# Opening of a one-level Strassen matmul with GELU: A11's first part as two halves, the first product over all row tiles per half of B12

## The chip, the cores and the metric

The kernel runs on one core of a Trainium2 chip. A core has TensorE for matrix products (PE, with PEld for its weight loads), VectorE (DVE), ScalarE (ACT), GpSimd (POOL) and SyncE (SP); POOL and SP issue the DMA transfers here. The metric is the device time of one execution in microseconds, lower is better, as the median of several runs.

## The reference

```python
def reference(a, b):                 # a, b: 4096 x 4096, float32, normal random
    x = np.matmul(a, b)
    return 0.5 * x * (1 + np.tanh(np.sqrt(2 / np.pi) * (x + 0.044715 * x**3)))
```

One product of 4096 x 4096 x 4096 and the tanh form of GELU on each element; the output is float32.

## The kernel before, in words

The operands are cast to fp16 on their way in and the products are accumulated in float32. Both matrices are cut into quadrants of 2048 x 2048, named by two digits: for A, "12" is the upper rows and the second half of the contraction; for B, the first half of the contraction and the right columns. The output is computed in 16 groups; a group is 512 rows and 512 columns of each of the four output quadrants. Instead of eight quadrant products most of the work uses seven products of sums and differences (`PRODUCTS`), and later groups use a second level of the same trick.

The first group is different, because nothing is on chip when it starts. For the first half of each quadrant's contraction (1024 of 2048, part 0) it computes the eight quadrant products plainly, in the order of `PLAIN`; for part 1 it uses the seven products. So the steps of the first group are 16 plain half steps (`plain(n)`, n = 0 to 15) and then 14 steps of `multiply` (line 581 is their matmul). A plain quadrant product is 512 x 512 outputs over 1024 of contraction: four row tiles i = 0 to 3 of 128 rows, each with eight matmuls of 128 x 128 by 128 x 512 (line 629), so 32 matmuls. The eight slices of the contraction are named (j, e), j = 0 to 3 and e = 0 or 1. A product is cut into its two half steps either by e (four matmuls for each of the four row tiles, then the other four) or, where `by_rows` is true, by row tiles.

What the opening has to bring in is written out by hand as words in a list (lines 731 to 750), each word under the number of the step before which it is issued:

- `A11_0` loads part 0 of A's quadrant 11 into a staging tile (`stage`), `B12_0` loads part 0 of B's quadrant 12 into its `bR` tile. All these loads are issued by POOL (line 485), in the order of the list. A load of an A part is 16 blocks of 32 rows; a load of a B part is two halves, e = 0 and e = 1.
- A suffix a or b is the first or second half (for A: row blocks 0 to 7 or 8 to 15; for B: e = 0 or e = 1), and p, q, r, s are quarters of A's row blocks (r: 8 to 11, s: 12 to 15). Every such piece is four DMA transfers, one for each 32 partitions. A half of either is 4 transfers of 128 KB, a quarter of A is 4 transfers of 64 KB (written bytes).
- `T11_0` transposes the staged rows into the `aT` tile on DVE (line 458); a suffix does it for these rows only. Row tiles 0 and 1 need T11_0a, row tile 2 needs T11_0r, row tile 3 needs T11_0s.
- `W11_0` squares and adds up the staged rows on ACT (line 494) for a guard on the numbers' size, in place, so it runs after the transposes, and the staging tile is free for the next load only after it.

The order of the words sets the order on each engine's queue; waits between engines come from what an instruction reads and writes. POOL also waits before an issue when too many of its transfers are under way (the planner of the later groups counts with `LANES = 8` on a queue).

Before the first product `warm()` runs `N_WARM` matmuls on zeros (line 590), so that TensorE is busy while the first data come in. In `plain`, the first product (n = 0 and 1: A11 by B12, output quadrant 12) has an order of its own: in n = 0 row tiles 0 to 2 take the four e = 0 slices, in n = 1 row tiles 0 to 2 take the four e = 1 slices, and then row tile 3 takes all eight. n = 2 and 3 are A11 by B11, n = 4 and 5 A21 by B11 (by rows), n = 6 and 7 A21 by B12 (by rows). When a product's accumulators are complete ACT copies them out (`keep`, line 599), or DVE adds them (line 595). The sums for `multiply` are made by DVE at line 566 (`make_sums`), two steps ahead.

From the second group on, a planner (`Plan`) orders all instructions at build time from fixed costs; the change does not touch its input.

Of the kernel before, what the change touches and what calls it, by code (L numbers as in the profile page):

```python
# [22 lines left out]
RT = 4  # L23
# [21 lines left out]
C21_FIRST = (0, 5, QPH - 1)  # L45
M5_FIRST = (1, 2, QPH - 1)
THIRD = ("22", 1)
N_WARM = 33

SQUARE_MAX = 2.0**22  # L50
SQUARE_MIN = 2.0**-6
# [295 lines left out]
def half_path(  # L347
# [225 lines left out]
    def bank(s, i):  # L573
        return PS[s][i][:, :]
# [11 lines left out]
    def warm():  # L586
        z = cell(sum_cells[0])
        nc.vector.memset(z[:, :NC], 0.0)
        for _ in range(N_WARM):
            nc.tensor.matmul(  # L590
# [3 lines left out]
    def tt(o, x, y, op):  # L594
        nc.vector.tensor_tensor(out=o, in0=x, in1=y, op=op)

    def keep(tag, src):
        t = ring(tag)[:, :]
        nc.scalar.copy(out=t, in_=src)
        return t  # L600

    def plain(n):

        (quad, oa, ob, by_rows), h = PLAIN[n // 2], n % 2
        seen = [x for x in range(len(PLAIN)) if PLAIN[x][0] == quad]
        sa, sb = a_phys[a_slot[oa], 0], b_phys[b_slot[ob], 0]
        sa = sa.rearrange("p jj (m e) -> p jj m e", e=2)
        tiles = [(j, e) for j in range(NJ // 2) for e in range(2)]
        odd = [[t for t in tiles if t[1] == e] for e in range(2)]
        rows = range(h * RT // 2, (h + 1) * RT // 2)  # L610
        if n == 0:
            pieces = [(i, odd[0]) for i in range(RT - 1)]
        elif n == 1:
            pieces = [(i, odd[1]) for i in range(RT - 1)] + [(RT - 1, tiles)]
        elif by_rows:
            pieces = [(i, tiles) for i in rows]
        else:
            pieces = [(i, odd[h]) for i in range(RT)]
        for i, part_ in pieces:
            begins, ends = part_[0] == tiles[0], part_[-1] == tiles[-1]  # L620
            acc = bank(0 if quad == "11" else 1, i)
            kept = quad == "11"
            start = (n // 2 == seen[0] or quad in ("12", "21")) and begins
            stop = (n // 2 == seen[-1] or not kept) and ends
            c = f"c{quad}"
            if quad == "22" and n // 2 == seen[1]:
                nc.scalar.copy(out=acc, in_=post.pop((c, i)))
            for j, e in part_:
                nc.tensor.matmul(
                    acc, sa[:, j, i * P : (i + 1) * P, e], sb[:, 2 * j + e, :],  # L630
                    start=start and (j, e) == part_[0], stop=stop and (j, e) == part_[-1],
                    skip_group_check=True,
                )
            if not stop:
                continue
            if quad in ("12", "21") and n // 2 == seen[1]:
                tt(post[c, i], post[c, i], acc, ALU.add)
            elif quad == "12":
                post[c, i] = keep("x1", acc)
            elif quad == "11":  # L640
                tt(post["c12", i], post["c12", i], acc, ALU.add)
            elif quad == "21":
                post[c, i] = keep("c21", acc)
            elif n // 2 == seen[0]:
                post[c, i] = keep("y", acc)
            else:
                tt(post["c12", i], post["c12", i], acc, ALU.subtract)
# [81 lines left out]
    before = {}  # L729

    for n, whats in (
        (0, "A11_0a B12_0a A11_0r B12_0b A11_0s T11_0a T11_0r T11_0s W11_0 B11_0 A21_0 A12_0 B22_0 B21_0"),
        (4, "T21_0 W21_0 A22_0"),
        (6, "T12_0 W12_0:0-8"),
        (8, "W12_0:8-16"),
        (10, "B12_1 A11_1 B22_1"),
        (11, "T22_0 W22_0 A12_1"),
        (13, "T11_1 A22_1 B21_1"),
        (16, "W11_1 B11_1"),
        (16, "T12_1"),  # L740
        (17, "A21_1"),
        (18, "T22_1 S2 W22_1:0-4"),
        (19, "W22_1:4-8"),
        (20, "W22_1:8-12"),
        (21, "W22_1:12-16"),
        (23, "T21_1"),
        (position[2, 2], "N11_0"),
        (position[3, 2], "N21_0"),
        (position[3, 3], "N11_1"),
        (position[4, 3], "N21_1"),  # L750
    ):
        for what in whats.split():
            half = what[-1] == "0" and what != "A11_0" and what[0] != "N" or what in ("A22_1", "T22_1")
            if what[0] == "S":
                before.setdefault(n, []).append((make_sums, (2, int(what[1]), "bS")))
                continue
            if what[0] == "N":
                before.setdefault(n, []).append((load, [(load_b1, (what[1:3], int(what[4])))]))
                continue
            if what[0] == "W":  # L760
                xs = range(*(int(x) for x in what[6:].split("-"))) if what[6:] else range(NX)
                before.setdefault(n, []).append((weigh_first, (what[1:3], int(what[4]), xs)))
                continue
            for h in (0, 1) if half else (None,):
                args = [
                    (x[0], (x[1:3], int(x[4]), x[5] if x[5:] in tuple("pqrs") else "ab".index(x[5]) if x[5:] else h))
                    for x in what.split("+")
                ]
                if what[0] == "T":
                    before.setdefault(n, []).append((turn_a, args[0][1]))  # L770
                    if what == "T22_1":
                        for q in range(QPH // 2, QPH):
                            before[n].append((make_sums, (2, q, "aS", h)))
                else:
                    pairs = [({"A": load_a, "B": load_b}[x], xs) for x, xs in args]
                    before.setdefault(n, []).append((load, pairs))

    def first_group():
        warm()
        table = pool.tile([P, 1], F32, name="table", tag="table")  # L780
        nc.vector.memset(table[:, :], 0.0)
        nc.scalar.activation(table[:, :], table[:, :], ACT.Gelu_apprx_tanh)
        for n, step in enumerate(steps):
            for fn, args in before.get(n, ()):
                fn(*args)
            if n + AHEAD < len(steps):
                s, q = steps[n + AHEAD]
                if s >= 0 and (0, *step) != C21_FIRST and (s, q) != M5_FIRST[1:]:
                    make_sums(s, q)
            if step[0] != 2:  # L790
                flush()
            combine()
            if step == (NP - 1, QPH // 2):
                for i in range(RT):
                    products(bank(0, i), *first_operands(), True, True, i)
            if step[0] < 0:
                plain(n)
            else:
                multiply(*step)
            if (0, *step) == C21_FIRST and n + AHEAD < len(steps):  # L800
                make_sums(*steps[n + AHEAD])
            if step == (2, QPH - 1):
                flush()
        flush()
        combine()
# [1352 lines left out]
def kernel(tc: tile.TileContext, a: bass.AP, b: bass.AP, out: bass.AP):  # L2158
    stands = half_path(tc, a, b, out)
    with tc.If(stands == 0):  # L2160
        general_path(tc, a, b, out)
# [30 lines left out]
```

## Time and profile before

| | before |
|---|---|
| median of 3 runs | 1450.55 us (1448.99 to 1450.82) |
| the profiled execution | 1450.24 us |
| its span in the trace | 1448.7 us |
| PE busy | 1436.2 us (99% of the span) |
| DVE / ACT / POOL busy | 1212.5 / 706.5 / 486.7 us |
| granted TensorE clock, mean | 1.00 |

The profiled execution is 0.31 us under the median of the runs, and 1.5 us of it lie outside the span. The views used below are: the page with its totals; PE's timeline, in which a row is a run of instructions with its start, its length, the count and, in brackets, how long the engine had been idle before and what ended that; the chain of waits, the work that ended last followed back from the end; the tables of busy time by window; and the list of DMA issues. A matmul's recorded time reaches to its modelled end, past the start of the next one, so a run of n matmuls takes (n - 1) spacings and one full record.

### The profile page before, as it was taken

How to read it: one execution, taken by the hardware profiler on the slowest of the kernel's cores; microseconds unless marked ns; L12 is line 12 of the kernel's file. 1: busy time of each engine (PE TensorE's matmuls, PEld its weight loads, DVE VectorE, ACT ScalarE, POOL GpSimd, SP SyncE). 2: the span in 40 equal slices, each digit the busy share in tenths (PEclk: the TensorE clock that was granted, in tenths of full speed). 3: DMA queues.
4: the chain of work that ended last, by engine and by line, in shares of the span. 5: the costliest groups of instructions: out<-in, count | busy, mean ns of one | idle time of the engine just before them, and what ended most of it. 6: DMA issues, size and time to landing. Idle time of an engine off the chain costs nothing.

```text
span 1448.7 us, 20127 instructions
## 1 busy us (share of the span) xinstructions
PE 1436.2 (99%) x6961; PEld 680.2 (47%) x6961; DVE 1212.5 (84%) x1315; ACT 706.5 (49%) x1480; POOL 486.7 (34%) x892
## 2 busy tenths in 40 slices
PE   8999999999999999999999999999999999999998
PEld 3444454564544545444444444444444444444443
DVE  2498988986878779989998989887998889887876
ACT  5645865455885543562655413453463622343133
POOL 8765251343244523331323343222322213111120
PEclk9999999999999999999999999999999999999999
DMA  9999999999999999998989899979898867775773
GB/s 160 195 218 241 300 267 276 245 276 255 235 241 246 259 286 234 285 286 285 307 289 323 262 311 320 290 221 343 225 345 251 303 224 265 281 267 204 268 257 116
DMA packets 205245, 378.94 MB, mean 262 GB/s; under 512 B 21072, under 2 KB 115792, under 8 KB 205136
## 3 DMA queue, kind: packets, MB, share of 16 engines
q0 software_dynamic: 146816, 245.42, 69.9%
q1 hardware_dynamic: 58320, 132.15, 24.3%
q8 instruction: 57, 0.93, 0.3%
q14 instruction: 52, 0.43, 0.1%
HBM read 333.45 MB, written 138.42 MB: 326 GB/s over the span
## 4 chain that ended last, share of the span: by engine, by line
PE 93%; DMA 3%; POOL 2%; DVE 1%; issue 1%; ACT 0%; DVEq 0%; POOLq 0%
PE acc L1857 58%; PE acc L581 30%; PE acc L1030 5%; DMA stage<-in_a_dram 2%; DMA bR<-in_b_dram 1%; POOL bR L485 1%; POOL stage L485 1%; DMA bR<-k_unit 0%; DVE y L1303 0%; DVE bR L945 0%; ACT stage L494 0%; DVE y L1388 0%; DVE aD L566 0%; POOL aD L485 0%; ACT y L2026 0%
## 5 line engine op out<-in xcount | busy, mean ns | idle before, releaser
L1857 PE MATMUL acc<-bR 128*128 128x512 f16 x1536 | 339.4, 379 | 0.9 <-DVE bR L945 0.9
L945 DVE TENSOR_TENSOR bR<-bR 128x2048 f16<-128x2048 f16 (+1 forms) x159 | 263.6, 1672 | 35.4 <-PE acc L1857 22.7
L826 POOL DMA_DIRECT2D bR<-k_unit x234 | 126.7, 543 | 491.0 <-PE acc L1857 364.1
L1857 PEld LDWEIGHTS <-bR 128*128 128x128 f16 x1776 | 173.5, 98 | 210.8 <-issue 1.1
L581 PE MATMUL acc<-bR,aT 128*128 128x512 f16 x1088 | 239.7, 379 | 0.9 <-DVE y L1303 0.9
L1857 PE MATMUL acc<-bR,aT 128*128 128x512 f16 x1008 | 223.6, 379 | 0.0
L1857 PEld LDWEIGHTS <-aT 128*128 128x128 f16 x1344 | 131.3, 98 | 158.8
L1869 ACT COPY acc<-acc 128x512 f32<-128x512 f32 x140 | 79.8, 570 | 245.8 <-PE acc L1857 229.6
L1303 DVE TENSOR_TENSOR y<-acc,y 128x512 f32<-128x512 f32 x251 | 166.2, 686 | 39.9 <-PE acc L1857 17.5
L826 POOL DMA_DIRECT2D bR<-in_b_dram x256 | 137.9, 544 | 180.8 <-PE acc L581 60.3
L581 PE MATMUL acc<-bR,aD 128*128 128x512 f16 x832 | 180.9, 379 | 0.0
L581 PEld LDWEIGHTS <-aT 128*128 128x128 f16 x1152 | 112.5, 98 | 132.6 <-issue 1.4
L1383 ACT ACTIVATE y<-bR 128x1024 bf16<-128x1024 f16 x128 | 130.6, 1051 | 70.4 <-DVE y L1388 62.7
L581 PEld LDWEIGHTS <-aD 128*128 128x128 f16 x928 | 90.6, 98 | 110.9 <-DVE aD L566 1.7
L1857 PE MATMUL acc<-bR,aD 128*128 128x512 f16 x624 | 138.4, 379 | 0.0
L1281 ACT ACTIVATE y<-y 128x512 f32<-128x512 f32 x160 | 98.4, 629 | 67.5 <-DVE y L1303 67.1
L1857 PEld LDWEIGHTS <-aD 128*128 128x128 f16 x784 | 76.6, 98 | 92.6
L1866 ACT COPY y<-acc 128x512 f32<-128x512 f32 x99 | 57.8, 585 | 93.3 <-PE acc L1857 87.8
L1388 DVE TENSOR_TENSOR y<-y 128x1024 bf16<-128x1024 bf16 x120 | 82.5, 688 | 23.8 <-ACT y L1383 22.4
L458 DVE STREAM_TRANSPOSE aT<-stage 128x1024 uint32<-128x1024 uint32 (+2 forms) x42 | 52.6, 1278 | 35.9 <-DMA stage<-in_a_dram 35.9
L1857 PE MATMUL acc<-stage,aT 128*128 128x512 f16 x336 | 75.6, 379 | 0.0
L826 POOL DMA_DIRECT2D stage<-in_a_dram x80 | 46.3, 586 | 69.6 <-ACT stage L1339 20.2
(124 smaller groups left out, 1670.8 us busy)
## 6 DMA issues: line engine op xcount, KB each, us to landing
bR<-k_unit POOLq DMA_DIRECT2D x234, 512.0 KB, 7.7
out_dram<-y SPq DMA_DIRECT2D x204, 256.0 KB, 7.1
bR<-in_b_dram POOLq DMA_DIRECT2D x352, 128.0 KB, 6.0
k_unit<-bR SPq DMA_DIRECT2D x76, 512.0 KB, 6.3
stage<-in_a_dram POOLq DMA_DIRECT2D x92, 256.0 KB, 9.7
stage<-k_unit POOLq DMA_DIRECT2D x46, 512.0 KB, 7.9
k_unit<-stage SPq DMA_DIRECT2D x28, 512.0 KB, 5.3
out_dram<-bR SPq DMA_DIRECT2D x46, 256.0 KB, 7.5
```

Of the source, the lines that this page charges most:

```text
L458: nc.vector.transpose(dst[:, :, x, :], src)
L581: nc.tensor.matmul(acc, sa[:, j // 2, i * P : (i + 1) * P, j % 2], sb[:, j, :], start=start and j == 0, stop=stop and j == 3, skip_group_c ...
L826: return plan.add(queue, COST[queue], lambda: eng.dma_start(out=dst, in_=src), r=r, w=w, size=MOVE[what] * SPREAD, weight=weight, **kw)
L945: nc.vector.tensor_tensor(out=dst, in0=xa, in1=ya, op=ALU.add if op > 0 else ALU.subtract)
L1030: nc.tensor.matmul(PS[s][i][:, :] if wide else PS[s][i][:, w * HC : (w + 1) * HC], sa[:, j // 2, r * P : (r + 1) * P, j % 2], rhs(j, wide) ...
L1281: act("gelu", lambda: nc.scalar.activation(t, t, ACT.Gelu_apprx_tanh), [("f", f)], [("f", f)])
L1303: dve("add", lambda: nc.vector.tensor_tensor(out=sm(g), in0=bank(s, i), in1=sm(f), op=ALU.add), [("f", f)], [("f", g), ("p", s, i)])
L1383: act("square", lambda t=t, src=src: nc.scalar.activation(t, src, ACT.Square), [c(cx)], [("f", f)], slack=60.0)
L1388: dve("add16", lambda t=t, u=u: nc.vector.tensor_tensor(out=u, in0=u, in1=t, op=ALU.add), [("f", f)], [("f", e)], slack=60.0)
L1857: nc.tensor.matmul(bank(w, i), sa[:, jx // 2, r * P : (r + 1) * P, jx % 2], bv[:, jx, :], start=p in "17" and jx == 0, stop=jx == NJ - 1, ...
L1866: act("copy", lambda: nc.scalar.copy(out=sm(f), in_=bank(w, i)), [("p", w, i)], [("f", f)])
L1869: act("copy", lambda: nc.scalar.copy(out=bank(*dst), in_=bank(*x)), [("p", *x)], [("p", *dst)])
```

## The change

Three edits.

1. The second half of A11's part 0 is loaded as one half in four transfers of 128 KB (`A11_0b`) where it was two quarters of four transfers of 64 KB each (`A11_0r`, `A11_0s`). The half stands where the first quarter stood, ahead of B12's second half; the second quarter stood behind it. The transposes keep their pieces: a half and two quarters.
2. The special order of the first product goes. n = 0 now takes the e = 0 slices for all four row tiles (16 matmuls; it was 12), n = 1 the e = 1 slices for all four (16; it was 20).
3. `warm()` issues 35 matmuls instead of 33.

```diff
-N_WARM = 33
+N_WARM = 35
...
         rows = range(h * RT // 2, (h + 1) * RT // 2)
-        if n == 0:
-            pieces = [(i, odd[0]) for i in range(RT - 1)]
-        elif n == 1:
-            pieces = [(i, odd[1]) for i in range(RT - 1)] + [(RT - 1, tiles)]
-        elif by_rows:
+        if by_rows:
             pieces = [(i, tiles) for i in rows]
         else:
             pieces = [(i, odd[h]) for i in range(RT)]
...
-        (0, "A11_0a B12_0a A11_0r B12_0b A11_0s T11_0a T11_0r T11_0s W11_0 B11_0 A21_0 A12_0 B22_0 B21_0"),
+        (0, "A11_0a B12_0a A11_0b B12_0b T11_0a T11_0r T11_0s W11_0 B11_0 A21_0 A12_0 B22_0 B21_0"),
```

## The prediction

> **What bounds the kernel now.** First the page:
>
> ```profile
> span 1448.7 us, 20127 instructions
> PE 1436.2 (99%) x6961; PEld 680.2 (47%) x6961; DVE 1212.5 (84%) x1315; ACT 706.5 (49%) x1480; POOL 486.7 (34%) x892
> PE 93%; DMA 3%; POOL 2%; DVE 1%; issue 1%; ACT 0%; DVEq 0%; POOLq 0%
> ```
>
> TensorE is busy for 99% of the span, yet 5% of the chain that ended last is DMA and POOL. So the second view is that chain, its first 85 us, and from a second answer its sequel:
>
> ```profile
> 11.70 2.13 POOL stage L485 x4
> 13.83 1.06 POOL bR L485 x2
> 14.89 5.18 DMA bR<-in_b_dram
> ...
> 42.69 1.31 ACT stage L494 x6
> ...
> 72.46 0.28 issue
> ...
> 79.43 4.17 DMA bR<-in_b_dram
> 83.61 1.24 DVE aD L566
> ```
>
> ```profile
> by line: PE acc L1857 61.5%; PE acc L581 31.7%; PE acc L1030 5.1%; DMA bR<-k_unit 0.4%; DVE y L1303 0.4%; DVE bR L945 0.2%; issue 0.1%; DVE y L1388 0.1%; DVE aD L566 0.1%; ACT y L2026 0.0%; DVEq L945 0.0%; DVEq L1388 0.0%
> ...
> 84.89 107.27 PE acc L581 x496
> ```
>
> Up to 83.61 the chain is almost only loads: POOL issues, a transfer lands, POOL issues again. From 84.89 on it is TensorE (98% of the rest), so what is won or lost at 84.89 should reach the end unchanged. The third view is PE's timeline up to there:
>
> ```profile
> 1.46 9.95 PE L590 MATMUL acc<-aD 128*128 128x512 f16 x33 [1.46 <-DVE table L781]
> 11.24 2.93 PE L629 MATMUL acc<-bR,aT 128*128 128x512 f16 x12
> 15.29 4.48 PE L629 MATMUL acc<-bR,aT 128*128 128x512 f16 x20 [1.12 <-DMA bR<-in_b_dram]
> 20.89 14.04 PE L629 MATMUL acc<-bR,aT 128*128 128x512 f16 x64 [1.12 <-DMA bR<-in_b_dram]
> 35.10 34.70 PE L629 MATMUL acc<-bR,aT 128*128 128x512 f16 x160 [0.17 <-ACT y L599]
> ...
> 76.61 7.07 PE L581 MATMUL acc<-bR,aD 128*128 128x512 f16 x32
> 84.89 13.99 PE L581 MATMUL acc<-aD 128*128 128x512 f16 x64 [1.21 <-DVE aD L566]
> ```
>
> 64 matmuls in 14.04 us are 63 spacings and one record of 0.38: 0.217 us each. A stall therefore costs its idle time plus 0.16, the part of a record that the next matmul would have covered. The costs: 0.18 inside the first twelve (2.93 instead of 11 x 0.217 + 0.38 = 2.76), 1.28 before 15.29 (waits for B12's second half), 1.28 before 20.89 (B11's first half), 0.33 before 35.10, 1.37 before 84.89 (a sum on DVE, which in the chain waits for a B load). Together 4.4 us: all that better loading can win behind the warm-up.
>
> The last one decides. Without it TensorE would go on at 83.52, so it has 1.37 us of slack against the load stream: the end moves with the moment at which the B load of 83.61 lands, not with what TensorE does at 11 to 20 us, until TensorE falls more than 1.37 us behind.
>
> **The change, part by part.** *Fewer, larger issues.* POOL's timeline and the list of issues:
>
> ```profile
> 6.13 1.11 POOL L485 DMA_DIRECT2D stage<-in_a_dram  x2
> 7.86 1.23 POOL L485 DMA_DIRECT2D stage<-in_a_dram  x2 [0.61 <-DMA stage<-in_a_dram]
> 9.20 2.50 POOL L485 DMA_DIRECT2D bR<-in_b_dram  x4
> 11.69 2.14 POOL L485 DMA_DIRECT2D stage<-in_a_dram  x4
> 13.82 4.29 POOL L485 DMA_DIRECT2D bR<-in_b_dram  x8
> 18.43 0.58 POOL L485 DMA_DIRECT2D stage<-in_a_dram  x1 [0.31 <-DMA bR<-in_b_dram]
> ```
>
> ```profile
> stage<-in_a_dram POOLq DMA_DIRECT2D x28, 128.0 KB, 5.0
> stage<-in_a_dram POOLq DMA_DIRECT2D x8, 64.0 KB, 3.8
> ```
>
> The quarters are the eight 64 KB issues at 6.13, 7.86 and 11.69, 0.535 to 0.58 us each; a 128 KB issue of the same kind took 0.58 (18.43). Four of 0.58 replace the first quarter's four (1.11 + 1.23 = 2.34), so B12's second half is still issued from about 9.2, and the four at 11.69 go: B11 and all loads behind it can be issued about 2.1 us earlier. Issue time is not landing time, so the windows:
>
> ```profile
> 8.00:10.00 2.00, 2.00 (x11) 0.93 (x10) 1.25 (x1) 0.34 (x2) 1.64 (x4) 1.00 1.25 192
> 10.00:15.00 5.00, 4.17 (x19) 1.52 (x17) 0.71 (x1) 4.66 (x24) 4.78 (x10) 1.00 1.20 165
> 15.00:20.00 5.00, 4.48 (x20) 1.88 (x20) 0.71 (x1) 2.50 (x10) 4.27 (x8) 1.00 1.06 144
> 20.00:30.00 10.00, 9.11 (x43) 4.17 (x44) 1.25 (x1) 3.67 (x16) 7.14 (x13) 1.00 1.38 193
> 30.00:84.00 54.00, 53.51 (x247) 23.82 (x245) 31.30 (x34) 33.92 (x146) 41.00 (x74) 1.00 1.32 196
> ```
>
> (Columns: window, length, busy us of PE, PEld, DVE, ACT and POOL with counts, granted clock, DMA share, GB/s.) From 20 us on the stream runs at 193 to 196 GB/s without a dip, so it is full, and a lead in bytes gained before 20 us is kept to 83.6. Between 10 and 20 us it is not full: 165 and 144 GB/s, while POOL is busy 4.78 and 4.27 of 5 us. Against 193 that is 5 x (193 - 165) + 5 x (193 - 144) = 385 KB, or 2.0 us of a full stream: the upper bound of the lead, near the 2.1 us of issue time. The lower bound is zero, and I let it go to -0.4 us, because the bytes are the same and the B11 transfers alone, eight 128 KB issues from 13.82, already meet a wait at 18.43 while the stream carries 144: there larger pieces do not fill it. I take the share that belongs to the quarters. 64 KB in 0.535 us is 122 GB/s; over 2.14 us that is (193 - 122) x 2.14 = 152 KB or 0.8 us short. The first quarter's issues are as slow, but the stream held 192 at 8 to 10 us, from what was queued; I add 0.2 us for them. **The lead: 1.0 us** (estimate from these rows).
>
> *The order of the bytes, and the first product.* B12's second half now has 262 KB more ahead of it, the second quarter's. The transposes and the T21 that matters later:
>
> ```profile
> 8.38 1.25 DVE L458 STREAM_TRANSPOSE aT<-stage 128x1024 uint32<-128x1024 uint32 x1 [6.97 <-DMA stage<-in_a_dram]
> 12.37 0.71 DVE L458 STREAM_TRANSPOSE aT<-stage 128x512 uint32<-128x512 uint32 x1 [2.74 <-DMA stage<-in_a_dram]
> 16.76 0.71 DVE L458 STREAM_TRANSPOSE aT<-stage 128x512 uint32<-128x512 uint32 x1 [3.68 <-DMA stage<-in_a_dram]
> ...
> 30.01 1.25 DVE L458 STREAM_TRANSPOSE aT<-stage 128x1024 uint32<-128x1024 uint32 x1 [2.57 <-DMA stage<-in_a_dram]
> ```
>
> A11's whole second half lands 262 KB after the first quarter did (12.37), at 165 to 193 GB/s 1.4 to 1.6 us: 13.8 to 14.0. Its two transposes end at 14.6 and 15.3, so row tile 2 waits about 1.1 us longer than row tile 0 and 1 last (to 11.67 + 8 x 0.217 = 13.4), and row tile 3 is done at about 16.2. B12's second half now lands where the second quarter did, 16.7, less a part of the lead: 16.2 to 16.7. Sixteen matmuls of 0.217 are 3.5 us, so n = 1 ends at 19.7 to 20.2. B11's first half, 20.89 before, comes at 19.9. So n = 2 starts at 19.9 to 20.2, 0.7 to 1.0 us earlier. Nothing is lost even if B12 came as late as 17.4 (3.5 before 20.89). ACT's squares of rows 8 to 11 start about 2 us later and those of rows 12 to 15 earlier; the copies of the first product behind them are needed only by n = 4, at about 27.
>
> *Before 35.10* TensorE waits for ACT's copies of quadrant 21's accumulators:
>
> ```profile
> 34.49 2.00 ACT L599 COPY y<-acc 128x512 f32<-128x512 f32 x4
> ```
>
> They stand behind the squares of A21, which follow T21's second half, released by a load at 30.01. That moves with the stream, TensorE's own part with n = 2: both 0.7 to 1.0 earlier. The chain's step through ACT at 42.69 (a staging tile free late) follows TensorE and moves as much.
>
> *Two more warm matmuls* end 0.43 us later, 11.67 instead of 11.24, for row tiles 0 and 1 alone; row tile 2 starts when its transpose lets it. They cost nothing; if that cover went, 0.43.
>
> *The sum.* The sum on DVE ends at 84.85 - 1.0; TensorE is there at 83.52 - 0.7 or earlier, so 84.89 becomes 83.9. 1450.24 - 1.0 = 1449.24. The profiled execution lay 0.31 under the median of the runs; half of that added gives **1449.4 us**, bounds of the lead alone 1448.2 (2.0) and 1450.6 (-0.4).
>
> **Rivals.** *Hidden.* The stream is full from 20 us, and its dip at 15 to 20 may belong to B11's access and not to the quarters: the wait at 18.43 speaks for it. Then the lead is within 0.4 us and the time 1450.3: the change does not do what it says. Against it: 165 GB/s at 10 to 15, while POOL is busy 4.78 of 5.
>
> *More.* The lead is over 1.8 us, because eight full transfers under way hold 193 GB/s from 8 us on. Then TensorE's other stalls shrink too: 1448.4 down to 1450.24 - 4.4 = 1445.8 if all go. Against it: n = 1 cannot end before 19.7.
>
> *The clock drops (slower).* Place: TensorE between 13.4 and 17 us. It now waits twice close together, about 1.1 us for T11_0r and up to 0.9 us for B12, with eight matmuls (1.7 us) between. The weight loads of the warm-up show the price:
>
> ```profile
> 3.56 0.15 PEld L590 LDWEIGHTS <-aD 128*128 128x128 f16 x1 [0.28 <-issue]
> 3.99 0.15 PEld L590 LDWEIGHTS <-aD 128*128 128x128 f16 x1 [0.28 <-issue]
> ...
> 6.92 3.98 PEld L590 LDWEIGHTS <-aD 128*128 128x128 f16 x19 [0.22 <-issue]
> ```
>
> 0.43 us apart until 6.92, then 0.216. A stretch as long as from 1.46 to 6.92 at half speed costs 2.7 us. It decides once TensorE loses more than the 1.37 us of slack: with the lead of 1.0, one stretch gives about 1450.6, two 1453.3, three 1456. Against it: stalls of 1.28 at 15.29 and 20.89 left the spacing at 0.217. [...]
>
> **How the numbers follow.** The forecast (lead 0.4 to 1.8) 0.58; hidden 0.22; more 0.10, of which 0.06 below 1447.65; the clock 0.10, of which 0.06 above 1453.45. 0.2% is 2.9 us, about what a measurement of this kernel can tell from no change; 4.4 us is all there is to win, so within 0.2% has 0.88, faster 0.06, slower 0.06. The forecast's own range is 1448.4 to 1449.9. The range for 8 in 10 takes in hidden, half of more and one cold stretch, with the runs' spread of about 1: 1447.4 to 1452.0.
>
> **What would show it.** B11's issues from about 11.7 to 12 instead of 13.82; over 170 GB/s at 10 to 20 us; n = 2 at 19.9 to 20.2; 84.89 at about 83.9; and a shift of the same size at the end. Wrong: a rate of 144 again at 15 to 20, a spacing of 0.43 after 13 us, or a stall after 84.89 that is not in the trace of before.

## The result, and the profile after

The changed kernel takes 1447.69 us (median of 14 runs, 1446.58 to 1450.05), the kernel before beside it 1450.23 us. The ratio is 0.9983 with a 95% interval of 0.9976 to 0.999: about 2.5 us or 0.17% faster, less than the 0.2% that the prediction took as its bound, but the interval excludes no change. On another chip the same pair gave 1447.93 and 1449.67 us, ratio 0.9988 (0.9979 to 0.9997).

The profiled execution took 1447.74 us, its span is 1446.1 us against 1448.7. PE's timeline of the changed kernel (start, length, line, operation, count, and in brackets the idle time before and what ended it):

```profile
1.46 9.36 PE L590 MATMUL acc<-aD 128*128 128x512 f16 x35 [1.46 <-DVE table L777]
11.14 1.89 PE L625 MATMUL acc<-bR,aT 128*128 128x512 f16 x8 [0.32 <-DMA bR<-in_b_dram]
14.61 53.81 PE L625 MATMUL acc<-bR,aT 128*128 128x512 f16 x248 [1.58 <-DVE aT L458]
...
75.16 7.07 PE L581 MATMUL acc<-bR,aD 128*128 128x512 f16 x32
82.46 13.99 PE L581 MATMUL acc<-aD 128*128 128x512 f16 x64 [0.23 <-DVE aD L566]
```

The three stalls of before inside the plain products (1.12, 1.12 and 0.17 us) are gone. A new one stands in their place, 1.58 us for the transpose of row tile 2, and the first product now waits 0.32 us for B12. From 14.61 on 248 matmuls run without a gap. The matmuls that started at 84.89 start at 82.46, 2.43 us earlier, and the stall before them is down from 1.21 to 0.23 us.

The stream of loads, by the same windows as before (columns as there; the last is GB/s):

```profile
3.00:8.00 5.00, 5.00 (x20) 2.06 (x19) 0.00 (x0) 0.00 (x0) 4.91 (x9) 1.00 1.14 144
8.00:10.00 2.00, 2.00 (x11) 0.88 (x9) 1.25 (x1) 0.65 (x3) 1.18 (x3) 1.00 1.14 169
10.00:15.00 5.00, 3.10 (x14) 1.12 (x13) 1.16 (x2) 3.07 (x17) 4.11 (x8) 1.00 1.34 195
15.00:20.00 5.00, 5.00 (x24) 2.17 (x23) 0.14 (x1) 4.52 (x18) 4.28 (x9) 1.00 1.23 201
20.00:30.00 10.00, 10.00 (x48) 4.52 (x47) 2.49 (x2) 4.74 (x22) 7.85 (x15) 1.00 1.43 194
```

The stream carries 195 and 201 GB/s at 10 to 20 us, where it had been 165 and 144. From 10 us on it is as full as later (194 at 20 to 30 us); only at 8 to 10 us it carries less than before, 169 instead of 192.

The shift at 82.46 does not reach the end unchanged. PE's waits after it, in the timeline of the changed kernel:

```profile
299.51 1.02 PE L581 MATMUL acc<-bR,aT 128*128 128x512 f16 x4 [0.92 <-DVE y L1299]
694.89 3.61 PE L1853 MATMUL acc<-bR 128*128 128x512 f16 x16 [1.23 <-DVE bR L941]
899.27 3.61 PE L1853 MATMUL acc<-bR 128*128 128x512 f16 x16 [0.47 <-ACT acc L1865]
```

Before, the second of these matmuls started at 696.96 after 0.86 us of idle time. So the lead is 2.43 at 299.5, 2.07 at 694.9, and a small stall at 899.3 that was not there takes 0.6 more. The last GELU on ACT ends at 1442.30; before, at 1443.74 (1443.08 and 0.66), 1.44 us later. The span gained 2.6 because what follows the last GELU, the last stores, took 3.8 us in this execution and 4.9 in that of before. In a second profile of the changed kernel the lead was 2.61 at 299.3, 2.16 at 694.8 and 2.16 at the last GELU. So the change brings 2.4 to 2.6 us at 84.9, and later waits take 0.4 to 1.0 of it. What follows the last GELU took 3.8, 4.9 and (in the second profile) 4.4 us, half a microsecond up or down. That the time fell by 2.5 us, as much as the lead, is therefore partly chance: between the first two profiles it is 2.43 of lead, less 1.0 at the waits, plus 1.1 in the tail. On the other chip it was 1.7.

### The profile page after: what moved, and what is told of

It reads as the page before. It is cut to its first block, busy times and chain, and to the rows that moved or that the text cites. A ratio compares the mean times of both kernels' runs of the same rounds, so it can differ in the third digit from the quotient of the medians.

```text
span 1446.1 us, 20123 instructions
## 1 busy us (share of the span) xinstructions
PE 1435.4 (99%) x6963; PEld 681.3 (47%) x6963; DVE 1212.2 (84%) x1315; ACT 707.0 (49%) x1480; POOL 485.7 (34%) x888
## 4 chain that ended last, share of the span: by engine, by line
PE 93%; DMA 3%; POOL 3%; issue 1%; DVE 1%; ACT 0%; DVEq 0%; POOLq 0%
PE acc L1853 58%; PE acc L581 30%; PE acc L1026 5%; POOL bR L485 2%; DMA stage<-in_a_dram 1%; POOL stage L485 1%; DMA bR<-in_b_dram 1%; DMA bR<-k_unit 0%; DVE y L1299 0%; DVE bR L941 0%; DVE y L1384 0%; DVE aD L566 0%; ACT y L1862 0%; POOL aD L485 0%; ACT stage L494 0%
## 5 line engine op out<-in xcount | busy, mean ns | idle before, releaser
L1862 ACT COPY y<-acc 128x512 f32<-128x512 f32 x99 | 57.9, 586 | 94.6 <-PE acc L1853 83.9
L1304 DVE TENSOR_TENSOR acc<-acc,y 128x512 f32<-128x512 f32 x100 | 67.9, 690 | 2.1 <-ACT acc L1865 1.1
```

The costliest lines, as they stand in the source:

```text
L1304: dve("add", lambda: nc.vector.tensor_tensor(out=bank(s, i), in0=bank(s, i), in1=sm(f), op=ALU.add), [("f", f)], [("p", s, i)])
L1862: act("copy", lambda: nc.scalar.copy(out=sm(f), in_=bank(w, i)), [("p", w, i)], [("f", f)])
```

## The experiments

Two theories stood against each other: that the eight 64 KB transfers leave the stream of loads short (S, later made exact as Q), or that it is the order of the bytes and products (O, P), or the B11 loads themselves (B), that make the dip at 10 to 20 us.

**Edit 1 alone.**

```diff
-A11_0a B12_0a A11_0r B12_0b A11_0s T11_0a
+A11_0a B12_0a A11_0b B12_0b T11_0a
```

> Edit 1 alone: A11's second half as four 128 KB transfers ahead of B12's second half; the first product's old order and 33 warm matmuls stay. Theory S (the eight 64 KB issues starve the load stream at 10 to 20 us; the order of the products plays no part): the whole shift comes with this edit, 195 GB/s or more at 10 to 20 us, the matmuls of 84.89 start at 82.3 to 82.8, time 2.2 to 2.8 us under the kernel before. Theory P (the gain needs the new order of the first product, since TensorE releases what follows): under half of that, 84.89 becomes 83.7 or later.

Measured: 1449.16 us, the kernel before 1449.90; ratio 0.9995 (0.9985 to 1.0004). PE's timeline, and the row of the windows:

```profile
11.10 1.89 PE L629 MATMUL acc<-bR,aT 128*128 128x512 f16 x8 [0.54 <-DMA bR<-in_b_dram]
14.56 1.04 PE L629 MATMUL acc<-bR,aT 128*128 128x512 f16 x4 [1.57 <-DVE aT L458]
16.41 52.82 PE L629 MATMUL acc<-bR,aT 128*128 128x512 f16 x244 [0.82 <-DMA bR<-in_b_dram]
...
82.89 13.98 PE L581 MATMUL acc<-aD 128*128 128x512 f16 x64
```

```profile
15.00:20.00 5.00, 4.18 (x20) 1.79 (x19) 0.09 (x1) 4.47 (x18) 4.27 (x9) 1.00 1.24 201
```

The stream is full (201) with edit 1 alone, and 2.0 of the 2.43 us at 84.89 are there. But now TensorE comes last at 82.89, with no wait in front of it: in the old order there are only four matmuls between row tile 2's transpose and B12's second half, and it stands idle for another 0.82 us. The new order puts row tile 3's four matmuls there. So P, which put these matmuls at 83.7 or later, is refuted there, and edit 2 is worth 0.3 to 0.4 us at this place. The time did not follow S, though: 0.7 us were gained, not 2.2 to 2.8. Between this kernel and the one with all edits but 33 warm matmuls (below) the medians of the runs show more, 1.5 us, than the two traces do (0.3 at 82.6, 0.8 in the span). Three of this kernel's ten runs show a mean granted clock of 0.998, against one in ten there. That the two stalls of 1.57 and 0.82 close together cost clock in those executions is a guess: in this kernel's trace the granted clock is 1.00 in every window from 0 to 84 us. The other seven have a mean of 1448.9, and where their remaining 1.2 us come from stays open. (An estimate: one stretch of 3.4 us at half clock, as in the last section, lowers the mean over the span of 1447.3 us by 0.0012, so a run listed with 0.999 can hold one too.)

**Edit 2 alone.**

```diff
-        if n == 0:
-            pieces = [(i, odd[0]) for i in range(RT - 1)]
-        elif n == 1:
-            pieces = [(i, odd[1]) for i in range(RT - 1)] + [(RT - 1, tiles)]
-        elif by_rows:
+        if by_rows:
```

> Edit 2 alone: the first product over all row tiles per half of B12, with the quarters and their place as before and 33 warm matmuls. Theory S: the stream is as before, 144 GB/s at 15 to 20 us; row tile 3 waits for the transpose that ends at 17.5, n = 1 ends at about 21.8, 0.9 us later than the B11 data that was waited for; the slack of 1.37 us at 84.89 swallows it: same time within 0.4 us. Theory P: 1 us or more faster.

Measured: 1451.52 us against 1449.90, ratio 1.0013 (1.0003 to 1.0023): slower by 1.6 us. PE's timeline and two windows:

```profile
11.55 2.75 PE L625 MATMUL acc<-bR,aT 128*128 128x512 f16 x12
17.45 54.53 PE L625 MATMUL acc<-bR,aT 128*128 128x512 f16 x244 [3.15 <-DVE aT L458]
...
85.62 13.98 PE L581 MATMUL acc<-aD 128*128 128x512 f16 x64
```

```profile
15.00:20.00 5.00, 2.55 (x7) 0.96 (x8) 0.71 (x1) 1.70 (x8) 4.12 (x8) 0.77 1.16 153
20.00:30.00 10.00, 10.00 (x45) 4.40 (x44) 2.12 (x2) 4.75 (x16) 8.12 (x15) 0.94 1.39 191
```

The wait for the second quarter's transpose is where S put it (17.45), and the stream has its dip (153). That the slack of 1.37 us would swallow it was wrong, because of a thing that S left out: after a stall of 3.15 us the granted clock is 0.77 and 0.94 in the next two windows. 244 matmuls took 54.53 us instead of 243 x 0.2165 + 0.38 = 53.0; these 1.5 us came on top, and TensorE arrived after the loads. Edit 2 without edit 1 is a loss.

**33 warm matmuls.**

```diff
-N_WARM = 35
+N_WARM = 33
```

> The changed kernel with 33 warm matmuls instead of 35. If the two cost and bring nothing: within 0.3 us of the changed kernel, first product from 11.14 as there (it waited 0.32 us for B12 behind 35 of them), spacing 0.217 from there on. If they hold the clock up: matmuls at 0.43 us after 11 us, and 1 to 3 us slower.

Measured, beside the changed kernel's other edits: 1447.70 us against 1449.90, ratio 0.9984 (0.9974 to 0.9994), the changed kernel's own ratio. The first product starts at 11.24 after 0.62 us of idle time (0.32 with 35), when B12's first half is there; the later matmuls start at 82.61. Edit 3 does nothing that can be seen.

**The quarters, in the new order of bytes.**

```diff
-A11_0a B12_0a A11_0b B12_0b T11_0a
+A11_0a B12_0a A11_0r A11_0s B12_0b T11_0a
```

> The changed kernel, its order of bytes and of products, but A11's second half as two quarters of 64 KB transfers, both ahead of B12's second half: 20 issues in the opening as in the kernel before, 4 more than in the changed one. Theory S (issue time and size): the stream is slow again, 140 to 170 GB/s somewhere at 10 to 20 us, all later issues about 2 us later, 84.89's matmuls at 84.3 to 84.9, time within 0.6 us of the kernel before. Theory O (the order of the bytes fills the stream, the size does not matter): 82.3 to 82.8 and the changed kernel's time.

Measured: 1450.53 us against 1449.90, ratio 1.0003 (0.9993 to 1.0012). The gain is gone. Windows and PE:

```profile
10.00:15.00 5.00, 4.38 (x20) 1.53 (x19) 1.42 (x2) 3.97 (x21) 4.50 (x9) 1.00 1.19 154
15.00:20.00 5.00, 2.48 (x11) 1.01 (x12) 0.00 (x0) 2.27 (x11) 4.14 (x9) 0.98 1.12 164
20.00:30.00 10.00, 10.00 (x41) 4.17 (x40) 1.48 (x2) 4.18 (x15) 8.08 (x15) 0.84 1.38 195
```

```profile
18.55 53.65 PE L625 MATMUL acc<-bR,aT 128*128 128x512 f16 x240 [2.52 <-DMA bR<-in_b_dram]
...
85.85 13.98 PE L581 MATMUL acc<-aD 128*128 128x512 f16 x64
```

Order, products and warm-up are those of the changed kernel; only A11's second half differs, eight transfers of 64 KB for four of 128 KB, and the dip is back. So it is the size, not the order. The first A21 transpose starts at 26.49 where the changed kernel has 24.37: the stream is 2.1 us behind. And again a stall (2.52 us) is followed by a lower clock (0.84), which puts the 85.85 behind the 84.9 expected. The drop alone does not explain the time: the three of the ten runs with a mean granted clock of 1.00 took 1449.0 to 1450.1 us.

Why the size matters so much is seen in the landings. Each transfer posts sixteen completions in the trace. The table has some of the opening's loads, numbered in order of issue: the start of the issue, the last completion, the time since the last completion of the transfer before, and issue to landing, all in us, worked out from the traces' semaphore events.

```
                     issue   landed   since   issue to landing
before   9  64 KB     6.13    11.20    0.33    5.06
        12  64 KB     8.54    12.24    0.35    3.70
        16 128 KB    11.15    15.16    0.76    4.01
        20  64 KB    13.29    16.64    0.43    3.35
        21 128 KB    13.82    18.14    1.50    4.32
        23 128 KB    14.89    20.08    1.07    5.19
changed  1 128 KB     1.55     4.72     -      3.17   (nothing ahead of it)
        12 128 KB     8.23    13.71    0.69    5.48
        16 128 KB    11.29    16.32    0.66    5.04
        20 128 KB    14.00    18.92    0.65    4.92
        24 128 KB    16.61    21.53    0.66    4.92
quarters 9  64 KB     6.13    11.66    0.36    5.53
        16  64 KB    11.59    14.09    0.33    2.51
        17 128 KB    12.12    15.47    1.38    3.35
        19 128 KB    13.18    17.76    1.63    4.57
```

When bytes are queued, a 128 KB transfer lands 0.65 to 0.69 us after the one ahead and a 64 KB transfer 0.33 to 0.36: the same 180 to 200 GB/s. A 128 KB transfer with nothing ahead of it took 3.17 us from issue to landing, so of the changed kernel's steady 4.92 some 1.8 us are queue (an estimate, the difference). POOL needs 0.54 us to issue 64 KB that land in 0.35. Every quarter therefore eats the queue, and when issue to landing is down at 2.5 to 3.4 us the next transfers come 1.1 to 1.6 us apart instead of 0.65. In the kernel before this happens at transfer 21, the first of B11: the dip at 15 to 20 us lies in the B11 loads, but the quarters issued just ahead of them made it.

The issue time is not the only reason. In all thirteen traces POOL never has more than eight of these loads under way: each issue starts at least 0.28 us after the landing of the load eight places ahead. In the changed kernel that wait, and not the issue time, sets the pace (transfer 12 landed at 13.71, transfer 20 was issued at 14.00). Where full 128 KB transfers land every 0.65 us, a quarter can be issued only every 0.65 us, and it brings half the bytes. Transfers 11 to 16 of the run above were issued 0.64 to 1.32 us apart for this reason; in the kernel before, the quarters of 11.69 to 13.29 came every 0.53 us, at the pace of issuing. Both eat the queue. No run allows more than eight under way, so how much belongs to which stays open.

**More quarters at the start.**

```diff
-A11_0a B12_0a A11_0b B12_0b T11_0a
+A11_0p A11_0q B12_0a A11_0b B12_0b T11_0a
```

> The changed kernel with A11's first half cut into two quarters of 64 KB transfers as well: 4 more issues, at the very start. Theory Q (a queue runs dry: a 64 KB transfer lands 0.35 us after the one before it but takes 0.54 us to issue, so quarters eat what is queued, and time is lost only when nothing is left): the first product's data come 0.5 to 1.2 us later, but B12 and the later loads lose only what the queue behind them cannot make up, 0.3 to 0.9 us; 84.89's matmuls at 82.8 to 83.4. Theory I (every issue of 0.54 us delays the whole stream by itself): all loads 2.1 us later, 84.3 to 84.6, the time of the kernel before.

Measured: 1449.22 us against 1449.80, ratio 0.9994 (0.9984 to 1.0004): most of the gain is gone. From 3 to 8 us the stream carries 107 GB/s, where the changed kernel has 144. PE:

```profile
13.02 1.89 PE L625 MATMUL acc<-bR,aT 128*128 128x512 f16 x8 [1.18 <-DMA bR<-in_b_dram]
16.49 53.80 PE L625 MATMUL acc<-bR,aT 128*128 128x512 f16 x248 [1.58 <-DVE aT L458]
...
84.64 13.99 PE L581 MATMUL acc<-aD 128*128 128x512 f16 x64 [0.53 <-DVE aD L566]
```

2.2 us later than the changed kernel, Theory I's number and not the 0.3 to 0.9 that I took for Q. This need not speak against a queue that runs dry, but my use of it was wrong. At the very start nothing is queued that could make up for slow issues: the first seven transfers of 64 KB took 2.4 to 3.1 us from issue to landing, no more than one with nothing ahead of it. So there each extra issue of 0.54 us delays everything by itself. This account was made after the run.

**Quarters where the stream is full.**

```diff
-B11_0 A21_0 A12_0
+B11_0 A21_0p A21_0q A21_0r A21_0s A12_0
```

> The changed kernel with A21's loads (issued from 17 us on, when the stream is full and eight transfers are under way) as four quarters of 64 KB transfers, 8 more issues. Theory Q: sixteen issues of 0.55 us are 8.9 us for bytes that land in 5.4; the queue of about 2 us behind the floor of 3 us from issue to landing takes up a part, so the stream falls 1 to 2 us behind with a dip in GB/s at 22 to 28 us; 84.89's matmuls at 83.3 to 84.3, time 0.5 to 1.8 us over the changed kernel. Theory B (the dip belonged to the B11 loads and the opening, not to small transfers): no dip, within 0.3 us of the changed kernel.

Measured: 1451.76 us against 1449.80, ratio 1.0007 (0.9997 to 1.0017), 4 us over the changed kernel's 1447.7 to 1447.9 (on two other chips). Windows and PE:

```profile
22.00:28.00 6.00, 5.20 (x25) 2.15 (x22) 1.15 (x1) 0.00 (x0) 4.95 (x10) 1.00 0.95 110
28.00:34.00 6.00, 5.84 (x28) 2.66 (x29) 1.34 (x2) 5.87 (x29) 5.60 (x11) 1.00 1.05 124
```

```profile
28.16 38.23 PE L625 MATMUL acc<-bR,aT 128*128 128x512 f16 x176 [0.95 <-DVE aT L458]
68.42 5.30 PE L625 MATMUL acc<-bR,aT 128*128 128x512 f16 x16 [2.04 <-ACT acc L623]
...
87.57 12.69 PE L581 MATMUL acc<-aD 128*128 128x512 f16 x58
```

No B11 load and no opening here, and the dip is deeper and longer than that of the kernel before: 110 and 124 GB/s over 12 us. Issue to landing falls from 4.92 to 3.10 us within six 64 KB transfers, and then the gaps begin. These six were issued 0.65 us apart, each behind the landing eight places ahead, so here it is the limit of eight and not the issue time that emptied the queue. Theory B is refuted. The price, 5.1 us at 87.57, is more than twice the upper end of what I gave to Q, since I had counted only the issue times, and neither the limit of eight nor what happens once the queue is empty. Of the 5.1 us the loads alone are 4.4 behind at 37 us, before the clock is at half from 69.2 to 72.6 us, behind the stall of 2.04.

**Fewer warm matmuls.** Three kernels, the changed one with

```diff
-N_WARM = 35
+N_WARM = 23      # and 28, and 16
```

> The changed kernel with 23 warm matmuls: TensorE stands idle from about 8.2 to 11.1 us, some 2.9 us, the length of the stalls after which the clock was seen at half in the two runs with a stall of 2.5 and 3.1 us. If the length of one stall decides: matmuls 0.43 us apart for a while after 11.1 and a granted clock of 0.5 to 0.8 there. If it took something else: 0.217 throughout.

> The changed kernel with 28 warm matmuls: a stall of about 1.8 us before 11.1, between the 1.58 us that left the clock at 1.00 and the 2.52 us after which it fell. If the length of one stall decides: clock 1.00, the changed kernel's time within 0.6 us. If stalls that follow each other add up (1.8 and then 1.6 us): half clock after 13 us.

> The changed kernel with 16 warm matmuls, so that TensorE stands idle for 2 us or more before the first product; 1.7 us had left the clock alone, while 2.04, 2.5 and 3.1 us elsewhere were followed by some 3 us at half. If the length of one stall decides: a granted clock under 0.9 in a window behind 11 us and matmuls 0.43 us apart there, 84.89's matmuls later than in the changed kernel only if TensorE loses more than its slack. If it needs more than one stall's length: 0.217 throughout.

With 23 and 28 the idle time before the first product came to only 1.68 and 1.73 us, each followed by the 1.58 for the transpose, and the clock stayed at 1.00; one execution each took 1447.27 and 1447.83 us. The first of the two therefore did not test what it was built for. With 16 it was 3.27 us:

```profile
10.86 58.38 PE L625 MATMUL acc<-bR,aT 128*128 128x512 f16 x256 [3.27 <-DMA bR<-in_b_dram]
...
82.88 13.98 PE L581 MATMUL acc<-aD 128*128 128x512 f16 x64
```

```profile
8.00:10.00 2.00, 0.00 (x0) 0.00 (x0) 1.25 (x1) 0.71 (x3) 1.71 (x4) 0.99 1.22 183
10.00:12.00 2.00, 1.14 (x3) 0.44 (x4) 0.00 (x0) 2.00 (x12) 1.41 (x4) 0.50 1.39 185
12.00:15.00 3.00, 3.00 (x8) 0.88 (x7) 1.30 (x2) 1.28 (x7) 2.42 (x5) 0.50 1.28 200
```

The clock is at half from 10 us on, for 6.8 us (an estimate from the granted clocks of 0.50, 0.50 and, from 15 to 20 us, 0.82). It cost only 0.4 us at 82.88 against 82.46 (1448.29 us in one execution), because the slow matmuls of the first rows fill the time in which TensorE would have waited for the transpose.

**A11 whole.**

```diff
-A11_0a B12_0a A11_0b B12_0b T11_0a
+A11_0 B12_0a B12_0b T11_0a
-N_WARM = 35
+N_WARM = 41
```

> A further step on the way of edit 1: A11's part 0 comes whole, in four transfers of 256 KB, ahead of both halves of B12; the transposes keep their pieces, the first product its new order, and 41 warm matmuls cover the longer wait. If what matters is that bytes are queued before the stream runs dry: the stream is full from about 5 us on (over 185 GB/s at 5 to 8 us, where it was 140 to 150), B12's second half lands about 1 us earlier, all four row tiles are transposed when the first product starts at about 12.3 and it runs without a stall, so TensorE and the stream are both about 0.7 us ahead of the changed kernel; 84.89's matmuls at 81.5 to 82, time 0.3 to 1 us under the changed kernel. If larger transfers do not help at the start: the first product starts at 13.5 or later, and the time is the changed kernel's or up to 0.8 us more.

> The changed kernel itself, beside the one with A11 whole on the same chip: 2.0 to 2.8 us under the kernel before, and how far the moment of 84.89's matmuls (82.46 in the first profile) differs from one execution to the next: within 0.4 us.

A11 whole: 1448.28 us, ratio to the kernel before 0.9993 (0.9984 to 1.0002); the changed kernel beside it 1447.93. No better, as far as this can tell. The changed kernel is 1.7 us under the kernel before here, less than the 2.0 to 2.8 expected; its matmuls of 84.89 start within the 0.4 us. PE of the first:

```profile
13.61 55.41 PE L625 MATMUL acc<-bR,aT 128*128 128x512 f16 x256 [1.27 <-DMA bR<-in_b_dram]
...
82.67 13.98 PE L581 MATMUL acc<-aD 128*128 128x512 f16 x64
```

The first product does run without a stall, and the wait for a B load before 84.89's matmuls is gone; but it starts at 13.61, not 12.3. The stream was not full from 5 us on (137 GB/s at 5 to 8): the second transfer landed 2.73 us after the first, and the window of 8 to 10 us is the first with 191. Between 28 and 78 us the loads do land about 0.9 us before those of the changed kernel, as was expected; TensorE, which started late, cannot use that. It then comes last at 82.67, 0.2 us after the changed kernel's 82.46 and 0.4 after the 82.28 of its second profile.

## Why the prediction was right or wrong

The time, 1447.69, lies inside the range, 0.3 us above its lower end, and 1.7 us under the value; the change is within the 0.2%. The likeliest case did not occur: the lead was 2.4 us and not 0.4 to 1.8, and the time lies outside the forecast's own 1448.4 to 1449.9. What came is the rival called *More*, to which I gave 0.10, and its reason, eight full transfers under way that hold the stream, is what the traces show from 10 us on. The range holds the time only because it took in half of *More*. Of the signs, B11's issues (from 11.94) and the rate came as said, 84.89 did not, and the shift at the end (1.44 us) is smaller than the one at 84.89. One sign of being wrong appeared: a stall after 84.89 that is not in the trace of before, 0.47 us at 899.27, though not in the second profile.

- *What bounds the kernel.* Held. The loads set the moment of 84.89, and the shift there is the shift of the stream. What I did not see is that a shift is not passed on in full: 0.4 to 1.0 us are lost at waits near 695 and, in one of two profiles, 899.
- *Fewer, larger issues: "The lead: 1.0 us".* This is the step that failed. The issue time saved (2.1) was near the lead measured, though in the changed kernel the landings and not the issue times set the pace of POOL. The loads led by 1.8 us at the last B11 transfer (21.53 against 23.35), 2.0 at 33 us and 2.4 at 75 us, so the upper bound from the windows (2.0) was about right for what was won by 20 us, and the lead was kept, as said, and grew a little. I then gave the dip at 15 to 20 us to the B11 loads, "there larger pieces do not fill it", and took only 0.8 + 0.2 us for the quarters. The runs show otherwise: with the quarters gone the B11 loads run at 201 GB/s, and with quarters in front of the A12 loads instead the dip is there. A starved queue shows later than its cause, by the 3 to 5 us from issue to landing; the quarters of 11.69 to 13.83 are the dip of 15 to 20. The 0.2 us for the first quarter was too little as well: over its four transfers issue to landing fell from 5.06 to 3.70 us, and it stood at 4.01 when the second quarter began.
- *The order of the bytes.* Held closely: the transposes of the second half at 13.84 (13.8 to 14.0 said), n = 2 at 14.61 + 24 x 0.217 = 19.8 (19.9 to 20.2 said). The stall before row tile 2 was 1.58 and not 1.1 us, since the first product began at 11.14.
- *Before 35.10.* Not as said: I let this stall of 0.17 us stay and move by 0.7 to 1.0 us on both sides. The transpose of A21's second half came 2.1 us earlier (27.87, it was 30.01) and TensorE only 1.1, so the stall is gone, and TensorE runs from 14.61 without a gap.
- *Two more warm matmuls.* Held: they cost nothing, and bring nothing.
- *The sum.* 83.9 said for 84.89, measured 82.46: the lead was 1.4 us more than its term. The waits near 695 and 899 and the shorter tail, neither of them in the sum, nearly cancel (1.0 against 1.1 us in the profiles), which is luck.
- *Hidden.* Refuted. *The clock drops.* It did not happen in the changed kernel, with 1.58 and 1.72 us as the longest stalls behind the warm-up in its two profiles. No run shows that two waits close together lower it: 1.73 and 1.58 us, with 1.9 us of matmuls between them, left it at 1.00. What four other runs show is matmuls at half rate behind stalls of 2.04, 2.52, 3.15 and 3.27 us.

## What to carry to other kernels

Where one engine issues many loads in a row, compare the time to issue one with the time between two landings when bytes are queued, and ask how many may be under way: in these runs a transfer that landed faster (0.35 us) than it was issued (0.54, or 0.65 where it waited for a full one to land) ate the queue, and the gap in GB/s appeared 3 to 5 us later, under the name of whatever was issued next. Take a dip in the stream as a question about the transfers issued before it, and test it by cutting another load that runs in a full stream into the same small pieces. An edit to the order of the products that costs on its own (edit 2: 1.6 us slower) may be right together with the edit that brings its data earlier.

## What the runs showed of the hardware that was not expected

The clock. Stalls of 2.04, 2.52, 3.15 and 3.27 us behind the warm-up were each followed by matmuls at half rate; after 1.72 us, and after 1.73 and 1.58 us with 1.9 us of matmuls between them, the granted clock stayed at 1.00 in the windows. The stretches at half behind these stalls are 3.4 us long, as estimated from the granted clocks in windows of 2 us: 0.93, 0.50 and 0.72 from 16 to 22 us with edit 2 alone, 0.94, 0.50 and 0.70 from 18 to 24 us with the quarters ahead of B12, 0.79, 0.50 and 0.85 from 68 to 74 us with the quarters where the stream is full. With 16 warm matmuls the stretch is twice that, 6.8 us (0.99, 0.50, 0.50 and 0.82 in the windows from 8 to 20 us). Three of the four begin late (estimates from the same windows): at 17.7, 19.8 and 69.2 us, while TensorE was busy again since 17.45, 18.55 and 68.42. With 16 warm matmuls, though, the half clock begins at about 10.0 us, inside the stall that lasts to 10.86.

What decides about a drop is not shown. In the thirteen traces the longest stall behind the warm-up that left the clock at 1.00 was 1.73 us, and the shortest that was followed by half rate 2.04. Whether a stall between the two, or a stall of the same length at another moment, would be followed by half rate was not measured.

The warm-up itself: 35 matmuls took 9.36 us, 33 had taken 9.95, and 28 took 7.74. In the trace the full clock is granted from 4.8 us on in the first and from 6.9 us on in the second; in a second profile of the first kernel it is 5.3. So the number of slow matmuls at the start differs from one execution to the next, also of the same kernel. In the traces of the kernel before and of the changed one the last of the sixteen parts of some transfers lands 0.4 us or more after the fifteenth, at most 1.36 us (transfer 35 before: 28.09 and 29.45) and 1.14 us (transfer 31 of the changed kernel). This is not explained, and such a late part can make up some of a gap between two last completions in the table.
